# An elementwise product and GELU on one core: which queue issues which of the first loads

## The chip, the core and the metric

The kernel runs on one core of a Trainium2 chip. The metric is the device time of one execution in microseconds (us); the time before is the median of three runs.

The engines that matter here: DVE (VectorE) multiplies, ACT (ScalarE) applies the GELU function, SP (SyncE) computes nothing and issues transfers. A transfer (DMA) is issued by an instruction on SP or on ACT; each of the two has its own queue of transfers, and 16 DMA engines move the bytes of both. Every transfer of this kernel has 128 rows, one for each partition of the on-chip memory, and each DMA engine has eight of them. A row is the piece of memory that one packet moves.

## The reference

```python
def reference(x, y):                       # both (1024, 4096) float32
    z = x * y
    return (0.5 * z * (1 + np.tanh(np.sqrt(2 / np.pi) * (z + 0.044715 * z ** 3)))).astype(np.float32)
```

Each of the two inputs has 16.78 MB, and so has the output: 50.33 MB move between the memory off the chip and the one on it.

## The kernel before

The 4,194,304 elements are seen as 128 partitions of 32,768 columns, and the columns are cut into three pieces (`PIECES`, line 14): piece 0 has columns 0 to 1280 (5,120 bytes in each partition, the "5 KB rows"), piece 1 has 1280 to 17664 (65,536 bytes, the "64 KB rows"), piece 2 has 17664 to 32768 (60,416 bytes). Each piece of each tensor is one contiguous block in the memory off the chip, and one transfer moves it.

All of x stays on the chip, in `xs`; the results replace it there. For y there isn't room: `ys` has 20,440 columns. The y loads (`Y_LOADS`, line 16) come in the order piece 1, piece 2, piece 0, and piece 2 and piece 0 overwrite columns that piece 1 had. In this text x0, x1, x2 are the x loads by piece, and y0, y1, y2 the y loads by their place in `Y_LOADS`: y0 is piece 1 (64 KB rows), y1 is piece 2, y2 is piece 0 (5 KB rows).

DVE works through the y loads in order (lines 90 to 108). Before each it waits for the x piece and the y load, then multiplies in steps (`STEPS`, line 20): four of 4096 columns, seven of 2048 and one of 768, and one of 1280. ACT applies the function to each step when DVE has done it (line 104). The semaphore `sem_mul` counts the multiplications, `sem_act` the activations.

The transfers are issued in an order written by hand. `_hoist` (line 25) takes an issue out of the kernel's body and puts it ahead of the barrier at which all engines meet at the entry. Line 79 does so with x0 on SP, line 80 with x1 on ACT. After the barrier SP issues y0 (line 81), x2 (line 82), then waits for three multiplications and issues y1, waits for a fourth and issues y2 (lines 83 to 86, `Y_FREE`). Then come the three stores (lines 110 to 114): the first waits for the landing of y1 and for the activations of piece 1, the others for the activations alone. After the entry ACT issues no transfers.

Of the kernel before, what the change touches and what calls it, by code (L numbers as in the profile page):

```python
# [1 line left out]

# [4 lines left out]


F32 = mybir.dt.float32
GELU = mybir.ActivationFunctionType.Gelu_apprx_tanh  # L10

PIECES = [(0, 1280), (1280, 17664), (17664, 32768)]

Y_LOADS = [(1280, 17664, 4056), (17664, 32768, 0), (0, 1280, 15104)]

Y_FREE = [0, 3, 4]

STEPS = [[4096] * 4, [2048] * 7 + [768], [1280]]  # L20
STORES = [(1280, 17664), (17664, 32768), (0, 1280)]
Y_BUF = 20440


def _hoist(nc, issued):

    here = nc.cur_bb.bb.instructions
    first = nc.main_func.blocks[0].instructions
    for ins in issued:
        del here[next(k for k, i in enumerate(here) if i is ins or i.name == ins.name)]  # L30
    engine = issued[0].engine
    at = next(
        k
        for k, i in enumerate(first)
        if i.engine == engine and type(i).__name__ == "InstDrain"
    )
    first[at:at] = issued


@with_exitstack  # L40
def kernel(
    ctx: ExitStack,
    tc: tile.TileContext,
    x: bass.AP,
    y: bass.AP,
    out: bass.AP,
):
    nc = tc.nc
    P = nc.NUM_PARTITIONS

    def columns(t, a, b):

        flat = t.flatten_outer_dims().rearrange("r c -> (r c)")
        pa, pb = next(q for q in PIECES if q[0] <= a and b <= q[1])
        return flat[P * pa : P * pb].rearrange("(p c) -> p c", p=P)[:, a - pa : b - pa]


    tc.close()
    tc.compile()  # L59

    xs = nc.alloc_sbuf_tensor("xs", [P, PIECES[-1][1]], F32).ap()
    ys = nc.alloc_sbuf_tensor("ys", [P, Y_BUF], F32).ap()
    sem_x = [nc.alloc_semaphore(f"sem_x{i}") for i in range(len(PIECES))]
    sem_y = [nc.alloc_semaphore(f"sem_y{i}") for i in range(len(Y_LOADS))]
    sem_mul = nc.alloc_semaphore("sem_mul")
    sem_act = nc.alloc_semaphore("sem_act")
    sem_o = [nc.alloc_semaphore(f"sem_o{i}") for i in range(len(STORES))]

    def load_x(i, engine=nc.sync):
        a, b = PIECES[i]  # L70
        return engine.dma_start(out=xs[:, a:b], in_=columns(x, a, b)).then_inc(sem_x[i], 16)

    def load_y(i):
        a, b, r = Y_LOADS[i]
        return nc.sync.dma_start(
            out=ys[:, r : r + b - a], in_=columns(y, a, b)
        ).then_inc(sem_y[i], 16)

    _hoist(nc, [load_x(0).ins])
    _hoist(nc, [load_x(1, nc.scalar).ins])  # L80
    load_y(0)
    load_x(2)
    for i in range(1, len(Y_LOADS)):
        if Y_FREE[i]:
            nc.sync.wait_ge(sem_mul, Y_FREE[i])
        load_y(i)

    n = 0
    done = {}
    for i, (a, b, r) in enumerate(Y_LOADS):  # L90
        for j, (xa, xb) in enumerate(PIECES):
            if xa <= a < xb:
                nc.vector.wait_ge(sem_x[j], 16)
        nc.vector.wait_ge(sem_y[i], 16)  # L94
        c = a
        for w in STEPS[i]:
            nc.vector.tensor_mul(  # L97
                out=xs[:, c : c + w],
                in0=xs[:, c : c + w],
                in1=ys[:, r + c - a : r + c - a + w],  # L100
            ).then_inc(sem_mul, 1)
            n += 1
            done[c + w] = n
            nc.scalar.wait_ge(sem_mul, n)
            nc.scalar.activation(  # L105
                out=xs[:, c : c + w], in_=xs[:, c : c + w], func=GELU
            ).then_inc(sem_act, 1)
            c += w

    for i, (a, b) in enumerate(STORES):  # L110
        if i == 0:
            nc.sync.wait_ge(sem_y[-2], 16)
        nc.sync.wait_ge(sem_act, done[b])
        nc.sync.dma_start(out=columns(out, a, b), in_=xs[:, a:b]).then_inc(sem_o[i], 16)
    for i in range(len(STORES) - 1):
        nc.sync.wait_ge(sem_o[i], 16)
    nums = sorted(s.num for s in [*sem_x, *sem_y, *sem_o[:-1], sem_mul, sem_act])
    assert nums == list(range(nums[0], nums[-1] + 1))
    nc.sync.sem_clear(range(nums[0], nums[-1] + 1))
    nc.sync.wait_ge(sem_o[-1], 16).then_inc(sem_o[-1], -16)  # L120


# [1 line left out]
_INS = ['x', 'y']  # L124
_OUTS = [((1024, 4096), 'float32')]


# [23 lines left out]
```

## Time and profile before

| what | value |
|---|---|
| time before, median of 3 runs | 119.97 us (119.89 to 119.98) |
| span of the profiled execution, first to last instruction | 118.3 us |
| first multiplication starts | 42.41 us |
| y1 issued, after the third multiplication | 55.54 us |
| DVE goes on with the first step of piece 2 | 78.10 us |
| first store issued | 78.02 us |

The span leaves out what lies before the first and after the last instruction; it is 1.7 us below the median of the runs. Times in the profile count from the start of the span. In its timeline the entry looks like this (start, length, engine, line; SPq and ACTq are the engines' queues of instructions, in which an issue takes the time shown and the transfer itself goes on afterwards):

```profile
0.00 0.39 SPq L71 DMA_DIRECT2D xs<-in_x_dram  x1
0.12 0.37 ACTq L71 DMA_DIRECT2D xs<-in_x_dram  x1
...
1.56 0.33 SPq L75 DMA_DIRECT2D ys<-in_y_dram  x1
1.57 1.28 ACT L105 ACT_TABLE_LOAD   x1 [1.57 <-PEq L59]
1.95 0.60 SPq L71 DMA_DIRECT2D xs<-in_x_dram  x1
```

The first two lines are the hoisted issues of x0 and x1; the third is y0, the last x2. The table load fetches what ACT needs for the function.

For each transfer the profile gives the time from the issue to the landing, that is until all 16 engines have reported it: 13.3 us for x0, 32.5 for x1, 40.7 for y0, 58.2 for x2, 22.5 for y1, 19.7 for y2, and 20.9, 20.4 and 20.8 for the stores in their order.

### The profile page before, as it was taken

How to read it: one execution, taken by the hardware profiler on the slowest of the kernel's cores; microseconds unless marked ns; L12 is line 12 of the kernel's file. 1: busy time of each engine (PE TensorE's matmuls, PEld its weight loads, DVE VectorE, ACT ScalarE, POOL GpSimd, SP SyncE). 2: the span in 40 equal slices, each digit the busy share in tenths (PEclk: the TensorE clock that was granted, in tenths of full speed). 3: DMA queues.
4: the chain of work that ended last, by engine and by line, in shares of the span. 5: the costliest groups of instructions: out<-in, count | busy, mean ns of one | idle time of the engine just before them, and what ended most of it. 6: DMA issues, size and time to landing. Idle time of an engine off the chain costs nothing.

```text
span 118.3 us, 82 instructions
## 1 busy us (share of the span) xinstructions
DVE 35.2 (30%) x13; ACT 31.0 (26%) x14; POOL 0.2 (0%) x4
## 2 busy tenths in 40 slices
DVE  0000000000000069999920000059999940000000
ACT  4000000000000001977974000007998990000000
POOL 0000000000000000000000000000000000000000
DMA  9888899889988897797797797798899889977975
GB/s 493 382 382 382 355 643 421 355 355 532 532 355 355 355 654 327 327 654 327 327 654 327 327 654 327 327 576 355 355 643 421 355 355 429 552 327 327 654 327 222
DMA packets 1296, 50.33 MB, mean 426 GB/s; under 512 B 144, under 2 KB 144, under 8 KB 528
## 3 DMA queue, kind: packets, MB, share of 16 engines
q1 hardware_dynamic: 1152, 41.94, 82.2%
q10 hardware_dynamic: 144, 8.39, 16.5%
HBM read 33.55 MB, written 16.78 MB: 426 GB/s over the span
## 4 chain that ended last, share of the span: by engine, by line
DMA 53%; DVE 24%; ACT 3%; issue 1%; DVEq 0%
DMA ys<-in_y_dram 53%; DVE xs L97 24%; ACT xs L105 3%; DVEq L94 0%
## 5 line engine op out<-in xcount | busy, mean ns | idle before, releaser
L97 DVE TENSOR_TENSOR xs<-xs,ys 128x2048 f32<-128x2048 f32 (+3 forms) x13 | 35.2, 2778 | 60.7 <-DMA ys<-in_y_dram 60.7
L105 ACT ACTIVATE xs<-xs 128x2048 f32<-128x2048 f32 (+3 forms) x13 | 29.7, 2301 | 64.9 <-DVE xs L97 64.9
L105 ACT ACT_TABLE_LOAD x1 | 1.3, 1283 | 1.6 <-PEq L59 1.6
L135 POOL MEMSET const-bfloat16-1.0<- 128x1 bf16 x1 | 0.1, 102 | 0.0
L135 POOL MEMSET const-uint8-127<- 128x1 uint8 x1 | 0.1, 102 | 0.0
L135 POOL MEMSET const-float32-0.0<- 128x1 f32 x1 | 0.1, 99 | 0.2 <-issue 0.2
L135 POOL MEMSET const-float32-1.0<- 128x1 f32 x1 | 0.1, 99 | 0.0
## 6 DMA issues: line engine op xcount, KB each, us to landing
xs<-in_x_dram SPq DMA_DIRECT2D x1, 7552.0 KB, 58.2
ys<-in_y_dram SPq DMA_DIRECT2D x1, 7552.0 KB, 22.5
out_dram<-xs SPq DMA_DIRECT2D x1, 7552.0 KB, 20.4
xs<-in_x_dram SPq DMA_DIRECT2D x1, 640.0 KB, 13.3
ys<-in_y_dram SPq DMA_DIRECT2D x1, 640.0 KB, 19.7
out_dram<-xs SPq DMA_DIRECT2D x1, 640.0 KB, 20.8
xs<-in_x_dram ACTq DMA_DIRECT2D x1, 32.5
ys<-in_y_dram SPq DMA_DIRECT2D x1, 40.7
```

The costliest lines, as they stand in the source:

```text
L97: nc.vector.tensor_mul(out=xs[:, c : c + w], in0=xs[:, c : c + w], in1=ys[:, r + c - a : r + c - a + w],).then_inc(sem_mul, 1)
L105: nc.scalar.activation(out=xs[:, c : c + w], in_=xs[:, c : c + w], func=GELU).then_inc(sem_act, 1)
L135: nc = _bacc.Bacc("TRN2", target_bir_lowering=False, num_devices=1)
```

## The change

x1, with 64 KB rows, is now the hoisted issue of SP, and y0, with 64 KB rows, that of ACT. After the barrier SP issues x2 (then y1 and y2 as before), and ACT issues x0, with 5 KB rows, ahead of its table load. The issues of y1, y2 and the stores, their waits, the steps of DVE and ACT and the layout stay the same.

```diff
-    def load_y(i):
+    def load_y(i, engine=nc.sync):
         a, b, r = Y_LOADS[i]
-        return nc.sync.dma_start(
+        return engine.dma_start(
             out=ys[:, r : r + b - a], in_=columns(y, a, b)
         ).then_inc(sem_y[i], 16)
 
-    _hoist(nc, [load_x(0).ins])
-    _hoist(nc, [load_x(1, nc.scalar).ins])
-    load_y(0)
+    _hoist(nc, [load_x(1).ins])
+    _hoist(nc, [load_y(0, nc.scalar).ins])
     load_x(2)
+    load_x(0, nc.scalar)
     for i in range(1, len(Y_LOADS)):
```

## The prediction

> **What bounds the kernel now.** I read the page's first two parts, then the chain of waits, the DMA issues, and the stretches of the trace around both ends.
>
> ```profile
> DVE 35.2 (30%) x13; ACT 31.0 (26%) x14; POOL 0.2 (0%) x4
> ...
> DMA  9888899889988897797797797798899889977975
> ...
> HBM read 33.55 MB, written 16.78 MB: 426 GB/s over the span
> ```
>
> Neither computing engine is busy for a third of the span, while the DMA row has no empty slice. 50.33 MB move. How close is 426 GB/s to what the transfers can do? The stretches answer (columns: from and to, length, busy time of DVE, ACT and POOL, clock, DMA share, GB/s). A packet's bytes are booked in the stretch in which it starts, so only long stretches show a rate.
>
> ```profile
> 0.90:1.00 0.10, 0.00 (x0) 0.00 (x0) 0.00 (x0) 1.00 0.00 0
> 1.00:1.10 0.10, 0.00 (x0) 0.00 (x0) 0.00 (x0) 1.00 0.98 358
> 1.10:1.25 0.15, 0.00 (x0) 0.00 (x0) 0.00 (x0) 1.00 0.97 341
> ...
> 1.75:2.00 0.25, 0.00 (x0) 0.25 (x1) 0.00 (x0) 1.00 0.86 348
> 2.00:2.10 0.10, 0.00 (x0) 0.10 (x1) 0.00 (x0) 1.00 8.90 3584
> 2.10:2.25 0.15, 0.00 (x0) 0.15 (x1) 0.00 (x0) 1.00 4.30 1782
> 2.25:2.50 0.25, 0.00 (x0) 0.25 (x1) 0.00 (x0) 1.00 4.56 1835
> ```
>
> ```profile
> 98.27:116.13 17.86, 0.00 (x0) 0.00 (x0) 0.00 (x0) 1.00 1.00 433
> 116.13:117.70 1.57, 0.00 (x0) 0.00 (x0) 0.00 (x0) 1.00 1.02 417
> ```
>
> Full rate is 433 GB/s, so 50.33 MB need 116.2 us. Nothing moves before 1.00 us. The last rows start by 117.7, take 0.2 us each (the 1.57 us of the last row shown are eight on each engine), and the span ends at 118.3, so some 0.4 us are completion. 1.0 + 116.2 + 0.4 = 117.6; the other 0.7 us are slips inside the stream. The kernel is one unbroken transfer of which only the first microsecond, the 0.7 us of slips and the end can be moved.
>
> The chain of waits seems to say otherwise:
>
> ```profile
> 1.56 40.75 DMA ys<-in_y_dram
> ...
> 42.41 13.11 DVE xs L97 x3
> 55.52 0.02 issue
> 55.54 22.47 DMA ys<-in_y_dram
> 78.00 0.03 issue
> ```
>
> It runs from the landing of y0 through three multiplications to the issue of y1. But an issue is not a start:
>
> ```profile
> xs<-in_x_dram SPq DMA_DIRECT2D x1, 7552.0 KB, 58.2
> ys<-in_y_dram SPq DMA_DIRECT2D x1, 7552.0 KB, 22.5
> ...
> xs<-in_x_dram ACTq DMA_DIRECT2D x1, 32.5
> ```
>
> x2, issued at 1.95, lands at 1.95 + 58.2 = 60.15. y1, issued at 55.54 on the same queue, lands at 78.0, which is 17.85 us after x2; its 7.73 MB at 433 GB/s are 17.86 us. So y1 didn't start until x2 was through; the issue had 4.6 us in hand. And x1 on ACT's queue landed at 32.6: from 1.0 to 32.6, 433 GB/s move 13.7 MB, of which x0 and x1 are 9.04, so 4.6 MB, over half of y0 on SP's queue, had moved beside x1. The two queues share the transfer engines.
>
> **The change, part by part.** (a) x0 leaves the front. Its 0.66 MB (the 1.57 us row above) no longer stand before x1 and y0. These are 16.78 MB, 38.75 us at 433, so from a start at 1.0 they end near 39.8 and land near 40.3 to 40.7 instead of 42.3. DVE starts 1.6 to 2 us earlier, its third multiplication ends near 53.7, and y1 is issued then. This is worth nothing at the end: y1 stands behind x2, and x0, x1, y0 and x2 are the same bytes, so x2 still lands near 60 and y1 near 78. The wait of 4.6 us behind x2 becomes 6.4. If that cover were gone (another order of the loads), 1.6 us would be the gain.
>
> (b) x0 goes behind y0 on ACT's queue. It shares with x2's rows after 40 us and lands before x2 does; the only reader is the last multiplication, which the tile view starts at 94.4: cover over 30 us, price nothing. Without it the same 1.57 us would stand elsewhere.
>
> (c) ACT issues one more DMA, right after the entry barrier (1.57 us) and ahead of its table load. 0.33 to 0.60 us, by the cheapest and dearest issue in the timeline; the table load moves from 1.57 to 2.0 or 2.2 and ends by 3.5. Its reader, the first activation, comes at 46.87 (then near 45), with the activations queued behind it: hidden by 40 us. SP loses one issue, y0's 0.33 us at 1.56; x2 is then issued at 1.56, and waits behind x1's rows until about 40: nothing. SP's waits for the multiplications stay where they are.
>
> (d) The first transfer on the empty machine is now SP's 64 KB rows in place of 5 KB rows. This is the one unknown price with a path to the end, because every microsecond before the first packet lengthens the stream. The trace has three starts. SP's 5 KB rows: issue begun at 0.00, packets at 1.00. SP's 64 KB store, behind other work: issue begun at 78.02, and 78.6 to 79.3 already has 64 KB rows starting (1608 GB/s), so 0.6 to 1.0 us. ACT's 64 KB rows: issue begun at 0.12, first packets at 2.00 (3584 GB/s can't be 5 KB rows; 16 rows of 64 KB start by 2.50), so 1.9 us. From the shortest, −0.4 us; from the longest, +0.9 us. I take 1.0 us, change zero: the same engine, the same place in the program, and the store shows that 64 KB rows on SP's queue need not be later; the 1.9 us I put down to ACT, or to its standing behind SP's descriptors, and y0 is in that place after the change too, under the cover of the first x1 row (64 KB on each of 16 engines, 1.05 MB, 2.4 us).
>
> A rule speaks to this point: the Trainium skill, "DMA: Bandwidth & Descriptors", section "Latency and other measured facts", gives about 0.6 us to the first byte of a DMA from the sync or scalar queue, without a word on row size. SP's x0 agrees (issue ended at 0.39, packets at 1.00); ACT's x1 does not (ended at 0.49, packets at 2.00). By the rule the changed kernel starts its stream at 1.0 us and the start is free; by the ACT row it loses 0.9 us.
>
> (e) The slip at the entry. The first rows of x0 start within 1.00 to 1.25; five rows per engine (410 KB) should take 0.95 us, yet the first x1 rows start over 2.00 to 2.50. The last engine has thus slipped 0.25 us more than the first while small rows and the late second queue overlapped, and its landings set all waits. With 64 KB rows from the start there is no such hand-over. Bounds: zero, if the slip comes with the start of any long row, and 0.5 us, the whole width. I take 0.25.
>
> The same page's section "Issuing engines are not separate DMA queues" speaks against any gain: issuing from several engines saves only the sequencer's time. The shared stream up to 32.6 us agrees, and by that rule the time would stay at 119.97.
>
> **Sum.** 118.3 + 0 (a, b, c, each hidden) + 0 (d) − 0.25 (e) = 118.05 us of span. The median of the runs, 119.97, lies 1.67 above the profiled span; the change touches nothing outside the span, so 118.05 + 1.67 = 119.72 us.
>
> **Rivals.** *Slow first rows* (the other side): the wait of 1.9 us belongs to 64 KB rows on an empty queue, not to ACT. Place: from the issue of x1 to its first packet. For it: the only 64 KB load whose start can be seen. Against: the store at 78.02. Price 0.9 − 0.25 = 0.65, so 120.6; it decides as soon as the first packet comes later than 1.25 us, when the gain of (e) is used up, and at 1.5 us it is slower than can be told from no change.
>
> *The slip comes back*: the 64 KB rows spread by 0.25 us themselves, and nothing changes: 119.97. For it: the rows that start over 2.00 to 2.50 are long rows. Against: they took over from engines that had already drifted.
>
> *The earlier DVE start reaches the end*: 1.6 us from (a), so 118.3. For it: the chain of waits as printed. Against: 17.85 us between the landings of x2 and y1.
>
> **How the numbers follow.** A measurement of this kernel can tell about 0.2% (0.24 us) from no change. The forecast has 0.48, with an own range of 119.45 to 119.95; it falls under 119.73 with 0.35 and within 0.2% with 0.13, since its middle lies close to the bound and its lower side reaches to the store's short start. Slow first rows 0.38: slower 0.35, within 0.2% 0.03 (a first packet between 1.25 and 1.5). The slip comes back 0.10, within. The DVE start 0.04, faster. Faster 0.39, within 0.26, slower 0.35. The range reaches from 119.4 (the store's start and my slip together, −0.4 − 0.25, would be 119.3, and I leave that corner out) to 120.75: the dear end of (d) is 120.6 with the gain of (e) and 120.9 without it, and between them no more than 2 in 10 is left out in all.
>
> **What would show it.** Right: first packets still near 1.00 and 64 KB rows from the first stretch on; DVE's first multiplication near 40.6; y1 issued near 53.7 and still landing near 78, some 24 us later; the last landing at 118.0. Wrong in (d): no bytes until 1.5 to 2.0 us, and every later landing late by the same amount. Wrong in (e): the first stretch as now, but x2's landing not before 60.1. Wrong in (a): y1 landing well before 77.

## The result, and the profile after

The changed kernel is slightly slower: 120.17 us (median of 22 runs, 119.94 to 120.29) against 119.89 (median of 22 runs of the kernel before beside it), a ratio of 1.002 with a 95% interval from 1.0012 to 1.0027. The profiled execution has a span of 118.9 us and itself took 120.29, the slowest of its 22 runs.

The chain of waits of the changed kernel (start, length, what):

```profile
0.12 41.44 DMA ys<-in_y_dram
...
41.67 13.11 DVE xs L97 x3
54.77 0.02 issue
54.79 23.89 DMA ys<-in_y_dram
78.68 0.03 issue
```

DVE started 0.7 us earlier than before and y1 was issued 0.75 us earlier. Neither reached the end: y1 took 23.9 us from issue to landing in place of 22.5, and landed at 78.68 in place of 78.0. From there the rest is the same in both. The first store, which waits for this landing, is issued at 78.70 here and at 78.02 before, and both spans end 40.2 to 40.3 us after that issue. So the 0.6 us between the two spans shown were lost before y1 landed (the medians lie 0.28 apart; more on this under e13).

The DMA issues show from where on the stream was late (last number: us from issue to landing):

```profile
xs<-in_x_dram SPq DMA_DIRECT2D x1, 7552.0 KB, 59.3
...
xs<-in_x_dram ACTq DMA_DIRECT2D x1, 640.0 KB, 59.4
...
xs<-in_x_dram SPq DMA_DIRECT2D x1, 41.4
ys<-in_y_dram ACTq DMA_DIRECT2D x1, 41.4
```

x1 and y0, issued at 0.00 and 0.12, both landed after 41.4 us. They are 16.78 MB, 38.75 us at 433 GB/s; from a start at 1.0 they should have landed near 40.2. More than 1 us was lost on the way. The stretches at the entry show where (columns as before: from and to, length, three engines' busy time, clock, DMA share, GB/s; a packet counts where it starts). First the changed kernel, then the kernel before:

```profile
0.90:1.00 0.10, 0.00 (x0) 0.00 (x0) 0.00 (x0) 1.00 0.00 0
1.00:1.25 0.25, 0.00 (x0) 0.00 (x0) 0.00 (x0) 1.00 9.03 2884
1.25:2.10 0.85, 0.00 (x0) 0.14 (x1) 0.00 (x0) 1.00 1.03 386
2.10:4.10 2.00, 0.00 (x0) 1.15 (x1) 0.00 (x0) 1.00 0.00 0
4.10:4.90 0.80, 0.00 (x0) 0.00 (x0) 0.00 (x0) 1.00 3.02 1311
```

```profile
1.00:2.00 1.00, 0.00 (x0) 0.43 (x1) 0.00 (x0) 1.00 0.95 374
2.00:2.50 0.50, 0.00 (x0) 0.50 (x1) 0.00 (x0) 1.00 5.35 2169
2.50:4.50 2.00, 0.00 (x0) 0.35 (x1) 0.00 (x0) 1.00 0.00 0
4.50:5.30 0.80, 0.00 (x0) 0.00 (x0) 0.00 (x0) 1.00 3.30 1413
```

Such lines give both the number of rows and their length in time. In the changed kernel 2884 GB/s x 0.25 us = 721 KB are 11 rows of 65,536 bytes, and 386 x 0.85 = 328 KB five more: the 16 first x1 rows, one for each DMA engine, started over 1.0 to 2.1 us. The share sums their durations: (9.03 x 0.25 + 1.03 x 0.85) x 16 engines = 50.1 us, or 3.13 us for a row. In the stream such a row takes 2.42 us (1.05 MB for 16 rows at 433 GB/s). No second row starts before 4.10, and by 4.90 all have (1311 x 0.80 = 1049 KB, 16 rows). Without loss this would have been at 3.4. So the engines are 0.7 to 1.5 us behind after a single row. The rows that start first are the slowest: 9.03 x 0.25 x 16 / 11 = 3.28 us for the eleven up to 1.25, 1.03 x 0.85 x 16 / 5 = 2.80 us for the five after it.

In the kernel before, 2169 x 0.50 = 1085 KB from 2.0 to 2.5 are 16 rows of 64 KB and seven of 5 KB; 5.35 x 0.50 x 16 = 42.8 us less 1.5 for the seven leaves 2.58 us for each long row. The first long rows after short ones are nearly as quick as in the stream.

### The profile page after: what moved, and what is told of

It is laid out like the page before. It is cut to its first block, busy times and chain, and to the rows that moved or that the text cites. A ratio compares the mean times of both kernels' runs of the same rounds, so it can differ in the third digit from the quotient of the medians.

```text
span 118.9 us, 82 instructions
## 1 busy us (share of the span) xinstructions
DVE 35.2 (30%) x13; ACT 31.0 (26%) x14; POOL 0.2 (0%) x4
## 3 DMA queue, kind: packets, MB, share of 16 engines
HBM read 33.55 MB, written 16.78 MB: 423 GB/s over the span
## 4 chain that ended last, share of the span: by engine, by line
DMA 55%; DVE 23%; ACT 3%; issue 1%; DVEq 0%
DMA ys<-in_y_dram 55%; DVE xs L97 23%; ACT xs L105 3%; DVEq L94 0%
## 6 DMA issues: line engine op xcount, KB each, us to landing
ys<-in_y_dram SPq DMA_DIRECT2D x1, 7552.0 KB, 23.9
xs<-in_x_dram ACTq DMA_DIRECT2D x1, 640.0 KB, 59.4
xs<-in_x_dram SPq DMA_DIRECT2D x1, 41.4
ys<-in_y_dram ACTq DMA_DIRECT2D x1, 41.4
```

## The experiments

All kernels change the entry, the waits or the sizes of pieces; where no result uses a load, its expectation says so. "Slip" is used for what the first rows lose. Each ratio is to runs of the kernel before that were made beside that experiment, so kernels of different experiments are better compared by their ratios than by their times. In the code shown, "..." marks lines left out. The distance from store issue to the end of the span was 40.2 to 40.3 us in all runs but e9 and e15 (40.5 to 40.6) and e12 (where the store is issued early), so the issue of the first store is the best measure of the entry.

### e1, e2: is it the power of two?

The 64 KB rows lie a power of two apart, and the 16 engines start together. Both kernels were run with 64 columns moved from piece 1 to piece 2.

```diff
-PIECES = [(0, 1280), (1280, 17664), (17664, 32768)]
+PIECES = [(0, 1280), (1280, 17600), (17600, 32768)]
...
-Y_LOADS = [(1280, 17664, 4056), (17664, 32768, 0), (0, 1280, 15104)]
+Y_LOADS = [(1280, 17600, 4120), (17600, 32768, 0), (0, 1280, 15168)]
...
```

> The changed kernel with piece 1 cut to 16320 columns, so that its rows are 65,280 bytes and lie 65,280 bytes apart in the memory off the chip instead of 65,536 (piece 2 gets the 64 columns). In the changed kernel the first x1 rows, on an idle machine, took a median of 3.2 us instead of 2.42, started over 1.0 to 2.03, and ended at 4.1 to 4.8. Theory A (the 16 engines start in step at addresses that are a power of two apart, and get in each other's way): the first rows start within 1.0 to 1.3, take 2.4 to 2.6 us, end by 3.9, and the kernel falls under the kernel before, to 119.4 to 119.8. Theory B (any long row on idle engines is slow to start): first rows take about 3.2 us as in the changed kernel, time 120.1 to 120.3. Theory C (ACT's descriptors for y0, written meanwhile, hold up SP's first rows): as B.

> The control: the kernel before, with the same piece sizes as e1_rows_65280_after (rows of 65,280 bytes). Theory A: the first x1 rows start behind five rows of x0, already out of step; a gain of 0 to 0.3 us on the kernel before, 119.6 to 119.9. Theories B and C: no change, 119.8 to 120.0.

Measured: the changed kernel with these rows 120.43 us, ratio 1.0048 (1.0035 to 1.0061) to the kernel before; the kernel before with them 119.81, ratio 1.0000 (0.9991 to 1.0009). The entry of e1:

```profile
1.00:1.25 0.25, 0.00 (x0) 0.00 (x0) 0.00 (x0) 1.00 7.65 2611
1.25:2.40 1.15, 0.00 (x0) 0.44 (x1) 0.00 (x0) 1.00 0.80 284
```

These are ten rows and five of 65,280 bytes, 3.0 us each (30.6 + 14.7 us for 15 rows; the sixteenth starts just before 1.00), over an even wider stretch. The distance of the rows is not the cause; theory A fell. That e1 is 0.26 us slower still than the changed kernel is not explained.

### e3: is it the new assignment of the queues?

```diff
-    _hoist(nc, [load_x(1).ins])
+    _hoist(nc, [load_x(0).ins])
     _hoist(nc, [load_y(0, nc.scalar).ins])
+    load_x(1)
     load_x(2)
-    load_x(0, nc.scalar)
```

> The changed kernel's queues, with the 5 KB rows of x at the front again: SP hoists x0 and issues x1 and x2 after the barrier, ACT hoists y0. If what stands first decides (A and B): the stream starts like the kernel before, packets at 1.0 and full rate from there, 119.8 to 120.0. If the new assignment of x to SP and y to ACT is the cost (rival Q): 120.1 to 120.3.

Measured: 119.87 us, ratio 1.0002 (0.9994 to 1.0010), first store issued at 78.38. x on SP and y on ACT cost nothing as long as x0's short rows go first. Its first long rows start only at 2.35, and take 2.5 us. What stands first decides. The Trainium skill, "DMA: Bandwidth & Descriptors", section "Issuing engines are not separate DMA queues", says that issuing from several engines saves only the sequencer's time to issue; that the exchange of the queues alone changes nothing, a ratio of 1.0002, agrees with it.

### e4: do y0's descriptors hold up the first rows?

```diff
-    _hoist(nc, [load_y(0, nc.scalar).ins])
+    load_y(0, nc.scalar)
```

> The changed kernel with ACT's y0 issued after the barrier (at about 1.5 us) instead of ahead of it. Theory C (y0's descriptors hold up the first x1 rows): the first x1 rows end by 3.9 us, time 119.6 to 119.9. Theories A and B: the first x1 rows take 3.2 us as in the changed kernel and end at 4.1 to 4.8; y0 has 2 us to spare, so the time is that of the changed kernel, 120.1 to 120.3.

Measured: 120.56 us, ratio 1.0057 (1.0038 to 1.0077). The first x1 rows start over 1.0 to 2.0 us and take 3.1 us each with no other transfer issued until 1.46. Theory C fell. The time is 0.4 us above the changed kernel's, which neither theory had, with 8 runs spread over 119.98 to 120.94; the store is issued at 78.85, 0.15 later.

### e5, e7, e8, e10, e11: what must stand ahead of the long rows?

With powers of two, queues and neighbours out, these put different short rows ahead of the changed kernel's x1. e5, e10 and e11 cut x1 in two, with a first part of 1280, 512 or 5120 columns; e7 and e8 load rows of 512 bytes that nobody uses.

```diff
...
-    _hoist(nc, [load_x(1).ins])
+    a, b = PIECES[1]
+    m = a + 1280                      # e10: 512, e11: 5120
+    _hoist(nc, [
+        nc.sync.dma_start(out=xs[:, a:m], in_=columns(x, a, m)).then_inc(sem_part, 16).ins,
+        nc.sync.dma_start(out=xs[:, m:b], in_=columns(x, m, b)).then_inc(sem_x[1], 16).ins,
+    ])
     _hoist(nc, [load_y(0, nc.scalar).ins])
...
+        if i == 0:
+            nc.vector.wait_ge(sem_part, 16)
...
```

```diff
...
-    _hoist(nc, [load_x(1).ins])
+    a = PIECES[0][0]                  # e8: PIECES[1][0]
+    _hoist(nc, [
+        nc.sync.dma_start(out=ys[:, 0:128], in_=columns(x, a, a + 128)).then_inc(sem_warm, 16).ins,
+        load_x(1).ins,
+    ])
     _hoist(nc, [load_y(0, nc.scalar).ins])
     load_x(2)
     load_x(0, nc.scalar)
+    nc.sync.wait_ge(sem_warm, 16)
...
```

> The changed kernel with x1 cut in two: SP hoists the first 1280 columns of piece 1 (5 KB rows, but 64 KB apart in the memory off the chip, like the long rows), and then the other 15104 columns. Power-of-two distances, ACT's descriptors and the assignment of the queues are out by the runs so far; what is left is that long rows are slow as the first ones. Theory L (the cost belongs to the length: short rows fill the first microsecond, as x0 does in the kernel before): the first 5 KB rows start within 1.0 to 1.5 us, take 0.2 to 0.4, and the time is 119.7 to 119.95. Theory P (the cost belongs to the place: rows spread over 8 MB answer late at first, x0's lie close together): these 5 KB rows take 0.5 to 1.5 us, the time is 120.1 to 120.5.

> The changed kernel with a small load ahead of x1 on SP: 128 rows of 512 bytes, 5 KB apart, read from x0's place into free columns of ys; no result uses it. If the DMA engines' own first use is the cost (theory U), it is paid by the small rows and the first x1 rows take 2.4 to 2.6 us; time 119.7 to 120.0. Theory P: the x1 rows behind it take 3 us or more; time 120.1 to 120.5. Theory L: 64 KB rows still come first in bytes (65 KB of small rows are 0.15 us of work), so x1's first rows are slow; 120.1 to 120.5.

> As the near warm-up, but the 512-byte rows are read from x1's place, 64 KB apart. Theory P: the small rows take the late answers on themselves (0.5 us or more each) and the x1 rows behind them take 2.4 to 2.6 us, the time between 119.8 and 120.2. Theory L: as with the near ones, small rows quick, x1's first rows slow, 120.1 to 120.5. Theory U: as near, 119.7 to 120.0.

> As e5_short_rows_of_x1, but the first part of x1 has 512 columns: eight rows of 2 KB for each engine, 16 KB or 0.6 us of work, between the 4 KB of the warm-ups (120.35) and the 40 KB of e5 (120.01). Theory L (short rows help by the work that they put ahead of the first long row): the first long rows take 2.6 to 2.9 us, time 120.05 to 120.3. If any 16 KB are enough: long rows 2.42 to 2.6 us, time 119.9 to 120.05. If only the number of rows counted: as e5.

> As e5_short_rows_of_x1, but the first part of x1 has 5120 columns: rows of 20 KB (0.76 us in a stream), 164 KB for each engine. If the length of the very first row is what costs: first rows of 1.0 to 1.5 us, spread starts, time 120.05 to 120.3. If it is enough that another row comes soon behind the first: as e5 or better, 119.8 to 120.05.

| rows ahead of the long ones | first store issued, us | time, us | ratio to before (95%) |
|---|---|---|---|
| none (the changed kernel) | 78.70 | 120.17 | 1.0020 (1.0012 to 1.0027) |
| e7, 512 bytes, near | 78.89 | 120.35 | 1.0037 (1.0024 to 1.0050) |
| e8, 512 bytes, wide | 78.83 | 120.34 | 1.0031 (1.0020 to 1.0043) |
| e10, 2 KB of x1 | 78.72 | 120.18 | 1.0034 (1.0021 to 1.0047) |
| e5, 5 KB of x1 | 78.37 | 120.01 | 1.0010 (1.0000 to 1.0020) |
| e11, 20 KB of x1 | 78.47 | 120.10 | 1.0026 (1.0015 to 1.0036) |

By the ratio e5 alone gains on the changed kernel, about half of what that lost, and even there the intervals overlap a little (that of e3, with x0's rows ahead, lies clear of it); e11 can't be told from the changed kernel, though its store is issued earlier. The entry of e7, with that of e8, settles three of the theories:

```profile
1.00:1.22 0.22, 0.00 (x0) 0.00 (x0) 0.00 (x0) 1.00 0.51 151
1.22:1.60 0.38, 0.00 (x0) 0.00 (x0) 0.00 (x0) 1.00 4.95 1637
1.60:2.30 0.70, 0.00 (x0) 0.00 (x0) 0.00 (x0) 1.00 1.74 655
```

1637 GB/s in the second stretch can only be 64 KB rows (nine, the rest being 63 rows of 512 bytes), and seven more start until 2.30. They are ACT's y0, and they are slow: (4.95 x 0.38 + 1.74 x 0.70) x 16 less 1.7 us for the short rows, over 16 rows, is 3.0 us each. The 512-byte rows themselves were quick (65 KB, out of the way within a microsecond, near and wide alike), and behind e8's wide ones the long rows take 3.0 us too. So the DMA engines' own first use (U) and the place of the rows (P) are out as the main cause: an engine that has just moved eight tiny rows is still slow with its first long one. e5's 5 KB rows, though 64 KB apart, help too, and then the first long rows take 2.5 us:

```profile
1.00:2.40 1.40, 0.00 (x0) 0.10 (x1) 0.00 (x0) 1.00 0.93 267
2.40:3.00 0.60, 0.00 (x0) 0.60 (x1) 0.00 (x0) 1.00 4.29 1807
```

(1807 x 0.60 = 1084 KB are 16 long rows and seven short ones; 41.2 us less 1.4, over 16.) Theory L holds for 0.5 and 5 KB. e11 shows that the help doesn't grow with the row: its first rows are slow themselves, the first of its two outcomes.

```profile
1.00:1.40 0.40, 0.00 (x0) 0.00 (x0) 0.00 (x0) 1.00 3.28 768
...
3.10:3.60 0.50, 0.00 (x0) 0.49 (x1) 0.00 (x0) 1.00 4.89 2097
```

768 x 0.40 = 307 KB are 15 rows of 20 KB, and 3.28 x 0.40 x 16 = 21.0 us are 1.40 for each, where the stream has 0.76; the 16 long rows behind them take 2.44 (4.89 x 0.50 x 16 = 39.1 us). e10 sits between in rows, but at the time of the changed kernel:

```profile
1.90:3.00 1.10, 0.00 (x0) 0.70 (x1) 0.00 (x0) 1.00 2.57 1018
```

Here 1018 x 1.10 = 1120 KB are 16 long rows and some 35 of 2 KB; 2.57 x 1.10 x 16 = 45.2 us less 4 leaves 2.6 us for a long row, nearly clean. But its short rows, 262 KB or 0.6 us of work from 1.0 on, kept the engines until 1.9 to 3.0 us: they took the slip instead. So part of the slip belongs to the first bytes whatever their rows, and 5 KB rows made it smallest among the sizes tried. The remainder of e5 to the kernel before, 0.15 us, can be its eight additional rows for each engine or the wider distance; that was not separated.

### e6, e9: the entry, or any start from idle?

e6 issues x1 and y0 after the barrier, e9 makes y1 wait until x2 has landed, so that the engines run dry in the middle of the kernel.

```diff
-    _hoist(nc, [load_x(1).ins])
-    _hoist(nc, [load_y(0, nc.scalar).ins])
+    load_x(1)
+    load_y(0, nc.scalar)
```

```diff
+    nc.sync.wait_ge(sem_x[2], 16)
     for i in range(1, len(Y_LOADS)):
```

> The changed kernel with x1 and y0 issued after the barrier instead of ahead of it, so that the first packet comes about 1.5 us later. Theory T (something else at the entry, up to some 2.5 us, takes the transfers' time, whatever they are): the first x1 rows start near 2.6 within 0.3 us and take 2.4 to 2.6; the time is 120.6 to 121.2 (1.5 us later, less what the slow start cost). Theories L and P: the first rows start spread over a microsecond and take about 3.2 us again; time 121.5 to 121.9.

> The changed kernel with one more wait on SP: y1 is issued only when x2 has landed, so that the DMA engines stand idle for about 1 us in the middle of the kernel and then all start with y1's long rows (60,416 bytes, 2.23 us each in the stream). Theory L in its wide form (long rows are slow whenever idle engines start with them): y1's first rows take 2.7 to 3.2 us and start over up to a microsecond; y1 lands 1.6 to 2.3 us later than in the changed kernel (78.7), time 121.8 to 122.6. Narrow form (only the program's first transfers are slow): y1's first rows take 2.23 to 2.35 us; y1 lands 1.0 to 1.4 us later, time 121.1 to 121.6.

Measured: e6 121.56 us, ratio 1.0130 (1.0113 to 1.0148); its first rows start at 2.4 to 3.2 and take 3.2 us (42.1 + 8.6 us over 16 rows). It is not something that is over by 2.5 us; theory T fell. e9 took 123.23 us. Its stretches around the dry place:

```profile
60.20:61.40 1.20, 0.00 (x0) 1.20 (x1) 0.00 (x0) 1.00 0.00 0
61.40:61.60 0.20, 0.00 (x0) 0.20 (x1) 0.00 (x0) 1.00 9.33 3021
61.60:62.30 0.70, 0.00 (x0) 0.70 (x1) 0.00 (x0) 1.00 1.60 518
62.30:64.30 2.00, 0.00 (x0) 0.16 (x1) 0.00 (x0) 1.00 0.00 0
64.30:65.40 1.10, 0.00 (x0) 0.00 (x0) 0.00 (x0) 1.00 2.03 879
```

Ten and six rows of 60,416 bytes start over 0.9 us and take (9.33 x 0.20 + 1.60 x 0.70) x 16 / 16 = 2.99 us each, where the stream has 2.23. This is the same picture as at the entry of the changed kernel, 60 us later and with another tensor, queue state and row length. So in the rows the wide form of L came: when all 16 engines start from idle with long rows, the first row takes some 0.7 us too long and the engines are spread by about a microsecond. The time of this single run lies above the range of either form, and y1 landed 2.6 us after the changed kernel's (81.3 against 78.7) where 1.6 to 2.3 were expected; a part of that is the gap itself.

### e12, e14, e15: a better version?

e12 lets the first store go without y1's landing; e14 issues x1 behind the barrier in the kernel before; e15 cuts its x1 into rows of 20 KB and the rest.

```diff
-        if i == 0:
-            nc.sync.wait_ge(sem_y[-2], 16)
```

```diff
-    _hoist(nc, [load_x(1, nc.scalar).ins])
+    load_x(1, nc.scalar)
```

```diff
...
-    _hoist(nc, [load_x(1, nc.scalar).ins])
+    a, b = PIECES[1]
+    m = a + 5120
+    _hoist(nc, [
+        nc.scalar.dma_start(out=xs[:, a:m], in_=columns(x, a, m)).then_inc(sem_part, 16).ins,
+        nc.scalar.dma_start(out=xs[:, m:b], in_=columns(x, m, b)).then_inc(sem_x[1], 16).ins,
+    ])
...
```

> The kernel before without the first store's wait for y1's landing: it is issued when piece 1 is activated (about 63.5 us) and stands behind y1 and y2 on SP's queue, so that no DMA engine waits for the slowest one's landing. If the spread between the engines costs time at this gate: 0.1 to 0.3 us faster than the kernel before, 119.55 to 119.75. If the slowest engine is never idle there and sets the end by its own stream: no change, 119.75 to 119.9.

> The kernel before with ACT's x1 issued after the barrier (about 1.5 us), so that all eight short rows of x0 stand ahead of the first long row instead of five. Theory L (short rows cover the first long rows' slow start, and five cover most of it): the first x1 rows take 2.42 to 2.6 us, the store is issued at 77.9 to 78.3, time 119.6 to 119.85. If the cover is used up and the engines run dry at 2.6 us before x1 is there: starts near 2.7 spread by half a microsecond again, 119.9 to 120.3.

> The kernel before with ACT's x1 cut in two: rows of 20 KB (5120 columns) first and the rest behind them, so that the rows grow from 5 to 20 to 60 and 64 KB. If growing rows start better than 5 KB followed by 64 KB: the last engine slips less than 0.5 us at the entry, the store is issued before 78.1, time 119.6 to 119.75. If eight more rows for each engine cost as much as that: 119.8 to 120.0.

All three lost. e12: 120.99 us, 1.0101 (1.0085 to 1.0116). With the stores right behind them, y2's eight rows for each engine are slow: y2 lands 21.2 us after its issue at 60.0, at 81.2, where the kernel before has it at 79.6 to 79.9. The wait that looks idle keeps stores out of the end of the loads; why the stores make these loads slower is not shown. e14: 121.61 us, 1.0148 (1.0133 to 1.0163). Here the long rows, issued only at 1.43, start behind all eight short rows, from 3.0 us on:

```profile
2.60:2.98 0.38, 0.00 (x0) 0.38 (x1) 0.00 (x0) 1.00 0.89 364
2.98:3.10 0.12, 0.00 (x0) 0.12 (x1) 0.00 (x0) 1.00 10.94 3909
2.98:4.10 1.12, 0.00 (x0) 0.14 (x1) 0.00 (x0) 1.00 2.65 950
4.10:5.70 1.60, 0.00 (x0) 0.00 (x0) 0.00 (x0) 1.00 0.00 0
```

2.65 x 1.12 x 16 = 47.5 us for 16 long rows and a few short ones: 2.9 us each. Its second outcome is the nearer one, but the time lies far above the 119.9 to 120.3 of it. And not all of these rows start from idle: until 2.98 the engines are busy with short rows for 0.89 of the time, and the seven long rows that start by 3.10 (3909 x 0.12 = 469 KB, with two short ones) take 2.9 us like the rest (10.94 x 0.12 x 16 = 21.0 us less 0.4). So short rows ahead are not enough by themselves, and what else the quick starts have, this run leaves open. e15: 127.22 us, 1.062 (1.0601 to 1.0638), by something else. The queues share by rows, not by bytes, so x1, now 16 rows for each engine in place of eight, got a smaller share beside the 64 KB rows of y0: y0 landed first, at 2.05 + 34.0 = 36.1 us, x1 at 0.53 + 51.1 = 51.6 (before: x1 at 32.6, y0 at 42.3), y1 was issued only at 64.82, and the stream stood dry from 60.2 to 65.7. The cover that part (a) of the prediction put at 4.6 us was used up. Neither expected outcome came in e12 or e15. None of the kernels tried beats the kernel before.

### e13: the kernel before, with its own time

> The kernel before, unchanged, with a profile of its own whose execution is timed. In the runs so far the time of a profiled execution is 1.35 to 1.39 us above its span. If the profile shown before the prediction (span 118.3) was a quick draw: this span is 118.4 to 118.7 and the time 1.3 to 1.4 above it. If the kernel before has another distance from span to time: 1.6 to 1.7.

Measured: 119.84 us, ratio 1.0002 (0.9993 to 1.0012); the profiled execution has a span of 118.5 and took 119.88, 1.38 above it, as the changed kernel's (118.9 and 120.29, 1.39). Its first store is issued at 78.29, its first long rows take 2.5 us. Its short rows, though, are not clean:

```profile
1.00:1.34 0.34, 0.00 (x0) 0.00 (x0) 0.00 (x0) 1.00 0.94 181
1.00:2.34 1.34, 0.00 (x0) 0.77 (x1) 0.00 (x0) 1.00 0.87 279
2.34:2.70 0.36, 0.00 (x0) 0.36 (x1) 0.00 (x0) 1.00 7.31 3012
```

The first 12 rows of 5 KB (181 x 0.34 = 62 KB) take 0.43 us each in place of 0.20, and 73 rows need 1.34 us, where the profile of before had as many in 1.00 (374 KB both times). So the kernel before has the slip at its start too, in its short rows, and by a different amount from execution to execution.

The profile that the prediction was made from (118.3, store at 78.02) was thus a quick draw, about 0.2 us under this one, and the difference of 0.6 between the two spans shrinks to 0.4 against e13. The medians differ by 0.28; the changed kernel's profiled execution was a slow draw.

## Why the prediction failed

*What bounds the kernel* was right. One unbroken transfer sets the time, and a gain or loss counts only at its ends or in its slips: 0.41 us more until the first store (78.29 to 78.70) are 0.41 us more in the profiled times (119.88 to 120.29).

*(a)*: the mechanism held. The earlier start of DVE was swallowed behind x2, and y1 landed 23.9 us after its issue, as forecast (some 24). The size was off, since the stream was late: the multiplication began at 41.67 and not near 40.6, y1 was issued at 54.79 and not 53.7.

*(b)* cost nothing, though x0 landed at 61.0 (1.57 + 59.4), with x2 and not before it; its reader comes 30 us later. *(c)* was right: the table load ran from 1.96 to 3.24, ahead of an activation at 46.13.

*(d)*: the value taken was right, the reading of its upper bound wrong. 64 KB rows on SP started at 1.00, as 5 KB rows had. What it left out is how such a row runs once it has started: the prediction took the wait for the first packet as the whole price of long rows on the empty machine, and the loss comes after that packet. The 1.9 us of ACT's x1 was no price of the rows or of ACT: in e7 ACT's 64 KB rows, issued at 0.12 likewise, start at 1.22, when the tiny rows ahead of them are few bytes. In the kernel before, the engines worked off five x0 rows each from SP's queue first (374 KB until 2.00 and seven rows after it are 80 rows, five for each engine).

*(e)* is the step that failed. I read the spread of the first x1 rows over 2.00 to 2.50 as damage done by small rows and a late second queue, and took 0.25 us as a gain from removing them. Its bounds reached only from zero to a gain. It is the other way round: without the short rows the loss at the entry grows. In the changed kernel the first long row takes 3.13 us, 0.71 more than in the stream. In e13 an engine's five short rows take 0.3 us too long together (0.87 x 1.34 x 16 / 73 = 0.26 us each in place of 0.20), and the long row behind them 0.12 (7.31 x 0.36 x 16 = 42.1 us, less 1.4 for seven short rows, over 16: 2.54). That is 0.4 against 0.7. The measured term is a loss, +0.28 us in the medians and +0.4 in spans. The trace of before couldn't show it: it had no start with long rows on idle engines, and its own clean start (374 GB/s in the first microsecond, where e13 has 279 over 1.34 us) was in part a quick draw.

*The sum* stood on a sound base for a wrong reason. The distance of 1.67 us was taken from a span and a median of different executions; in one execution it is 1.38 (e13), and the other 0.3 were a profiled execution quicker than the usual one. Since both were added to the same sum, its base was the median, 119.97 (119.89 in the 22 runs). The error of (e) is 0.53 us, 0.25 of gain in place of 0.28 of loss; the base, 0.08 too high, makes the whole error 0.45 (119.72 against 120.17).

*The rivals*: the one on the slow side had the right side and the wrong mechanism. It asked for a first packet after 1.25 us; the first packet came at 1.00, and the loss lies in how the first row runs. That 120.17 lies within the stated 119.4 to 120.75 is luck: the upper part of that range was there for this rival's wait, which did not occur. *The slip comes back* was the nearest in kind, but expected the same slip and not a larger one. The rule of the Trainium skill on the time to the first byte ("DMA: Bandwidth & Descriptors", section "Latency and other measured facts", about 0.6 us) agrees with the first packets at 1.00, and says nothing of how quickly the first row then moves.

What stays open is why the first rows are slow. The runs show where it happens (engines starting from idle with rows of 20 KB or more, and e14's long rows) and what makes it smaller (five 5 KB rows ahead, with the long ones issued at the entry as well), not what the engines wait for in that time. Nor is it settled whether it belongs to the row, to the first microsecond or so after a start, or to the time since the issue: the slow first rows of e10, e11 and e13 and the quicker late starters of the changed kernel speak for the second, e14 against it. The extra 0.26 and 0.4 us of e1 and e4 are open too.

## What to carry to other kernels

In a kernel that is one long stream of transfers, try short rows first, some microsecond of them on every DMA engine, even if nobody needs them soon, with the long ones issued beside them. Here it was 5 KB rows that helped, by 0.1 to 0.2% of the time; 0.5, 2 and 20 KB did not. And the stream should never run dry, because the price is the gap and a slow first row on top (e9). If a wait or a load looks wasteful in such a kernel, ask what it keeps apart before taking it away.

## What was not expected of the hardware

- The first long row from idle: 3.0 to 3.2 us in place of 2.42 (64 KB; the changed kernel, e1, e4, e6, e7) and 2.99 in place of 2.23 (60,416 bytes, e9), with starts spread over 0.7 to 1.4 us. First rows of 20 KB took 1.40 in place of 0.76 (e11), the first of 5 KB 0.43 in place of 0.20 in one execution (e13) and 0.2 in another. Eight rows of 512 bytes ahead of the long ones left these slow.
- Each DMA engine took five 5 KB rows from one queue before its first row from the other, two of 20 KB in e11, and all eight of 512 bytes or 2 KB (e7, e10): ACT's rows could start at 1.22 (e7) but started at 2.0 behind x0. From then on the queues took turns row by row, so that a queue with smaller rows gets fewer bytes (e15).
- Loads that end while stores stand right behind them were slow in the one kernel that had this: y2, 0.66 MB, landed at 81.2 in place of 79.6 to 79.9 (e12).
